# Forgetting attention with 64-row score matmuls, one division on ScalarE and early exponential tables; latent attention with the second head's queries ahead of the first exponentials

## The chip, the core and the metric

The program runs on one core of a Trainium2 chip. The metric is the device time of one execution in microseconds (us); lower is better. The changed kernel is timed against the kernel before on the same chip.

## The reference, cut to what matters

The model is two decoder layers on 256 rows of width 1024. Layer 0 mixes with forgetting attention (16 heads of 64), layer 1 with latent attention (16 heads). Each layer has two gated feed-forward halves around the mixer and a gated input embedding behind them, with a layer norm after each step.

```python
def fox_mixer(x, w_in, b_f, w_o):
    h = x @ w_in                      # queries, keys, values, and 16 gate logits
    cum = jnp.cumsum(jax.nn.log_sigmoid(f_logit), axis=1).transpose(0, 2, 1)
    s = jnp.einsum('bqhd,bkhd->bhqk', qb, k) * FOX_HEAD_DIM ** -0.5
    s = s + cb[:, :, :, None] - cum[:, :, None, :]     # then causal softmax, times v, times w_o
def mla_mixer(x, w_dq, q_norm, w_uq, w_o, k_nope, k_rope, v, cos, sin):
    c_q = rms_norm(x @ w_dq, q_norm)
    q = jnp.einsum('bsc,chd->bshd', c_q, w_uq)         # 128 plain and 64 rotated columns a head
    s = jnp.einsum('bqhd,bkhd->bhqk', qn, k_nope) + jnp.einsum('bqhr,bkr->bhqk', qr, k_rope)
for i in range(DEPTH):
    x = post_norm(x, 0.5 * swiglu(x, ffn1_w_in[i], ffn1_w_out[i]), ln_g[i, 0], ln_b[i, 0])
    ...
```

## The kernel before, in words

**Number format.** Every product is made of three float32r matmuls: both operands are split into a high part (a copy on ScalarE that rounds) and a low part (a subtraction on VectorE), and the products high-high, high-low and low-high are added up in PSUM. `parts` does it for an activation, `Stream.split` for a weight that a DMA has brought into a `raw` buffer. So each block of weights costs ScalarE and VectorE one pass each before TensorE can use it.

**What sets the order.** The engines' programs are written out by hand: what stands earlier in the code is earlier in each engine's queue, and an engine works through its queue in order. Only the weight splits are placed by a planner: `pump`, called after every three matmuls, puts the next split in if its own estimate of the engines' clocks allows. `S.hold` forbids that. A split can be cut in two (`ahead`, `later`): its ScalarE half is queued at one place (L172) and its VectorE half at another (L176). PSUM has three rings of banks: `y` (4), `h` (2) and `tr` (2).

**Forgetting attention** (`fox`, L807). The values and the gates come first. The gate chain (`s1`, `s2`, `s3`) uses an exponential (L859) and a logarithm (L866) on ScalarE, then sends the sums of the logarithms through DRAM and back as `fall`, and masks it on GpSimd (`mask_fall`, L898). Heads are worked in 8 pairs j. For each pair: `gen_k` makes the keys of two heads in 128 rows (head 0 in rows 0 to 63, head 1 in 64 to 127), `gen_q` the queries; `QK` the scores; `softmax` the bias and row minimum (VectorE, L952), four exponentials with their sums (ScalarE, L962), the reciprocals of the sums (VectorE, L969), four divisions (GpSimd, L973); `T` transposes the weights on TensorE (L986, L471), `AV` multiplies by the values. The loop (L1033) issues, on TensorE: `gen_k(j+1)`, `T(j-1)`, `QK(j)`, `gen_q(j+1)`, `AV(j-1)`. Behind the loop come the output products `O`, a block of queries at a time, the first block's layer norm, and the transposes `XT(0)` of the normed block, ahead of the last `O(7, 1)`.

**The scores before.** The keys are kept in `kz` with zeros in the other head's rows (two memsets, L845 and L846, and four half copies, L918 and L920), so that one matmul over all 128 rows gives both heads:

```python
for n, (i, jj) in enumerate(((0, 0), (0, 1), (1, 0))):
    self.mm(pairs(sb[0][:, 0:256]), q[:, i, 0:128], pairs(k[:, jj])[:, :, 0:128], n == 0, n == 2)
for n, (i, jj) in enumerate(((0, 0), (0, 1), (1, 0))):
    self.mm(sb[1], q[:, i, 128:256], k[:, jj], n == 0, n == 2)
```

**Latent attention** (`mla`, L1146). The query latent is normed in `dq` (`rms_scale`: a square with sum on ScalarE, L1089; mean plus epsilon on GpSimd, L1090; a power on GpSimd, L1091; the scaling on VectorE, L1165). Then come values `V`, rotated queries `q_rope` and `rotate`, and their transposes `rope_T`. Heads are worked one by one: `QK(h)`, `softmax(h)` (VectorE, L1288), `T(h-1)`, `exps(h)` (ScalarE, L1297), `divide(h)` (VectorE L1305, GpSimd L1307), and `gen(h+1)` (`gen_k`, `gen_q`: keys and queries of the next head in one bank, split into `qk`). For head 0 the keys of head 1 are made ahead of the loop, and `gen_q(1)` stands behind `divide(0)`. Two blocks of values, `V(2, 0)` and `V(2, 1)`, are split just ahead of the loop into a tile of the ring `g4` (g in the trace) and into `qq`.

Of the kernel before, what the change touches and what calls it, by code (L numbers as in the profile page):

```python
# [10 lines left out]
F32 = mybir.dt.float32  # L11
F32R = mybir.dt.float32r
AF = mybir.ActivationFunctionType
ALU = mybir.AluOpType
# [367 lines left out]
class Trunk:  # L382
# [33 lines left out]
    def setup(self):  # L416
        nc = self.nc
        one = lambda shape, dt, name: self.tl(shape, dt, name, 1)
        self.x = [one([128, D], F32, f"x{t}") for t in range(2)]
        self.ident = one([128, 128], F32, "ident")  # L420
        self.mask = one([128, 384], F32, "mask")
        self.mhalf = one([128, 1], F32, "mhalf")
        self.xT = one([128, 2, 2, 8, 128], F32R, "xT")
# [11 lines left out]
        nc.gpsimd.memset(self.mhalf, -0.5)  # L435
        nc.scalar.activation(warm, self.mhalf, AF.Silu)
# [370 lines left out]
    def fox(self, li):  # L807
# [39 lines left out]

        f, e, u, r, ab = (fs[fr, 256 * i : 256 * i + 256] for i in range(5))
        sc = fs[:, 1280:1536]
# [2 lines left out]
        def gates():  # L852
# [56 lines left out]
        st, PT = {}, {}  # L909
        OT = [self.own([128, 4, 2, 256], F32R, tag) for tag in ("ota", "otb")]  # L910

        def gen_k(j):
            ps = self.bank("h")
            ws(("fk", j), ps[:, 0:256], {0: S.split_now} if j >= 2 else {}, j >= 2)
            o = kz[:, j % 2]
            part = [(slice(64 * s, 64 * s + 64), slice(256 * s, 256 * s + 256)) for s in range(2)]
            for r, c in part:
                nc.scalar.activation(o[r, 0, c], ps[r, 0:256], AF.Copy)  # L918
            for r, c in part:
                nc.vector.tensor_tensor(o[r, 1, c], ps[r, 0:256], o[r, 0, c].bitcast(F32), op=ALU.subtract)  # L920
            self.S.busy(act=600, dve=600)

        def gen_q(j):
            ps = self.bank("h")
            ws(("fq", j), ps[:, 0:256], {}, j >= 2)
            o = qq[:, j % 2]
            self.parts(o[:, 0, :], o[:, 1, :], ps[:, 0:256])

        def QK(j, ring):
            sb = [self.bank(ring) for _ in range(2)]  # L930
            q, k = qq[:, j % 2], kz[:, j % 2]
            pairs = lambda ap: ap.rearrange("p (s c) -> p s c", s=2)
            for n, (i, jj) in enumerate(((0, 0), (0, 1), (1, 0))):
                self.mm(
                    pairs(sb[0][:, 0:256]), q[:, i, 0:128], pairs(k[:, jj])[:, :, 0:128], n == 0, n == 2
                )
            for n, (i, jj) in enumerate(((0, 0), (0, 1), (1, 0))):
                self.mm(sb[1], q[:, i, 128:256], k[:, jj], n == 0, n == 2)
            st[j] = sb

        def softmax(j):
# [5 lines left out]
            seg = ((0, 128), (128, 384))  # L947
            S2 = [[sb[q][:, w * s : w * s + w] for q, w in enumerate((128, 256))] for s in range(2)]
# [21 lines left out]
            for s in range(2):  # L970
                for q, (c0, c1) in enumerate(seg):
                    i = 2 * s + q
                    nc.gpsimd.tensor_scalar(  # L973
                        P[s][:, c0:c1], P[s][:, c0:c1], su[:, i : i + 1], 1.0, op0=ALU.mult, op1=ALU.mult
                    )
            if j < 7:
                mask_fall(j + 1)
            st[j] = P

        def T(j):  # L980
# [39 lines left out]
        gen_q(0)  # L1020
        y = [[None] * 2 for _ in range(2)]

        def O(k, t):
            w = self.use(("fo", k))
            if k == 0:
                y[t] = [self.bank("y") for _ in range(2)]
            for n in range(2):
                self.mm3(
                    y[t][n], lambda i: OT[k // 4][:, k % 4, i, 128 * t : 128 * t + 128],
                    lambda i: w[:, i, 512 * n : 512 * n + 512], k == 0, k == 7,  # L1030
                )

        for j in range(8):  # L1033
# [16 lines left out]
            softmax(j)  # L1050
            if j < 7:
                gen_q(j + 1)
            else:
                O(2, 0)
                S.split_now()
                O(3, 0)
            if j >= 1:
# [26 lines left out]
    def rms_scale(self, src, n, junk):  # L1084
# [61 lines left out]
    def mla(self, li):  # L1146
# [116 lines left out]
        def gen(h):  # L1263
            gen_k(h)
            gen_q(h)
# [111 lines left out]
        rope_T(0, 0)  # L1377
        split_v = V(2, 0, "y", later=True)
        rope_T(1, 0)
        if not self.rec:  # L1380
            split_v()
        V(2, 1, "y", "qq")
        for h in range(16):
            S.hold = True
            QK(h)
            softmax(h)
            if h >= 1:
                T(h - 1)
            exps(h)
            if h >= 1:  # L1390
                T_low(h - 1)
            divide(h)
            if h == 0:
                gen_q(1)
            elif h < 15:
                gen(h + 1)
            S.hold = False
            if h == 0:
# [118 lines left out]
```

## Time and profile before

| | |
|---|---|
| median of 3 runs | 1081.13 us (1080.95 to 1082.05) |
| profiled execution, its own time | 1080.49 us |
| its span, first to last instruction | 1078.7 us |
| TensorE matmul busy | 1064.0 us (99%), 7050 matmuls |
| VectorE busy | 711.2 us (66%) |
| ScalarE busy | 541.8 us (50%) |
| GpSimd busy | 86.9 us (8%) |
| read from HBM | 199.95 MB, 186 GB/s over the span |

The busy time of TensorE says little by itself, since a matmul's end is modelled and overlaps its successor. The useful reading is the time from the start of one group of matmuls to the start of the next: it shows what a group costs, and where TensorE stood still. PEld is TensorE's loading of weights, DVE is VectorE, ACT is ScalarE, POOL is GpSimd. A row of the timeline has the start, the length of the merged group, engine, line, operation, tiles, shapes and count, and in brackets the idle time before it with what ended it. Consecutive rows of one engine that do the same are merged, also across two weights.

### The profile page before, as it was taken

How to read it: one execution, taken by the hardware profiler on the slowest of the kernel's cores; microseconds unless marked ns; L12 is line 12 of the kernel's file. 1: busy time of each engine (PE TensorE's matmuls, PEld its weight loads, DVE VectorE, ACT ScalarE, POOL GpSimd, SP SyncE). 2: the span in 40 equal slices, each digit the busy share in tenths (PEclk: the TensorE clock that was granted, in tenths of full speed). 3: DMA queues.
4: the chain of work that ended last, by engine and by line, in shares of the span. 5: the costliest groups of instructions: out<-in, count | busy, mean ns of one | idle time of the engine just before them, and what ended most of it. 6: DMA issues, size and time to landing. Idle time of an engine off the chain costs nothing. (4 is left out here: it accounts for less than half of the span.)

```text
span 1078.7 us, 17453 instructions
## 1 busy us (share of the span) xinstructions
PE 1064.0 (99%) x7050; PEld 966.6 (90%) x7050; DVE 711.2 (66%) x979; ACT 541.8 (50%) x797; POOL 86.9 (8%) x143
## 2 busy tenths in 40 slices
PE   9999999999999999999999999999999999999996
PEld 6989999889889989998899898988999889898985
DVE  5765545778797545458977454488886985454567
ACT  5564433557656435453555343345766474444431
POOL 0000000333300000000330000011111100000000
PEclk9999999999999999999999999999999999999998
DMA  9886653455358866545387564344473678555502
GB/s 286 283 295 228 198 193 98 157 196 197 96 173 281 266 229 195 195 144 188 104 297 264 195 196 158 98 106 132 147 221 127 196 248 289 187 181 188 187 1 78
DMA packets 151616, 202.14 MB, mean 187 GB/s; under 512 B 12000, under 2 KB 128752, under 8 KB 151536
## 3 DMA queue, kind: packets, MB, share of 16 engines
q1 hardware_dynamic: 151536, 201.04, 56.9%
q8 instruction: 55, 0.90, 0.3%
q14 instruction: 25, 0.20, 0.1%
HBM read 199.95 MB, written 1.06 MB: 186 GB/s over the span
## 5 line engine op out<-in xcount | busy, mean ns | idle before, releaser
L165 DVE TENSOR_TENSOR hl<-raw,hl 128x1024 fp32r<-128x1024 f32 (+3 forms) x286 | 330.1, 1174 | 160.6 <-ACT hl L164 159.4
L164 ACT ACTIVATE hl<-raw 128x1024 fp32r<-128x1024 f32 (+3 forms) x286 | 283.9, 1017 | 196.3 <-PE y L467 85.5
L467 PE MATMUL h<-xT,hl 128*128 128x256 f32 x2064 | 242.4, 277 | 0.0
L467 PEld LDWEIGHTS h<-xT,hl 128*128 128x128 f32 x2064 | 238.7, 188 | 0.7
L467 PE MATMUL y<-hl,g 128*128 128x512 f32 x804 | 186.6, 390 | 0.0
L467 PEld LDWEIGHTS y<-hl,g 128*128 128x128 f32 x804 | 150.1, 188 | 30.7
L467 PE MATMUL tr<-xT,hl 128*128 128x256 f32 x840 | 98.9, 277 | 0.0
L467 PEld LDWEIGHTS tr<-xT,hl 128*128 128x128 f32 x840 | 96.9, 188 | 0.1
L467 PE MATMUL h<-hl,xT 128*128 128x512 f32 (+1 forms) x396 | 94.5, 388 | 0.9 <-DVE hl L165 0.9
L467 PEld LDWEIGHTS h<-hl,xT 128*128 128x128 f32 x396 | 71.9, 188 | 17.2 <-DVE hl L165 2.7
L539 POOL TENSOR_TENSOR rs<-ve,mhalf 128x1 f32<-128x1 f32 x16 | 15.2, 950 | 820.3 <-DVE ve L538 806.7
L467 PE MATMUL y<-hl,xT 128*128 128x512 f32 (+2 forms) x276 | 57.8, 363 | 0.0
L467 PEld LDWEIGHTS y<-hl,xT 128*128 128x128 f32 x276 | 47.5, 188 | 7.4
L477 DVE TENSOR_TENSOR g<-P,g 128x512 fp32r<-128x512 f32 x36 | 24.9, 693 | 34.5 <-ACT g L476 34.5
L476 ACT ACTIVATE g<-P 128x512 fp32r<-128x512 f32 x36 | 22.7, 632 | 40.0 <-DVE P L646 29.0
L165 DVE TENSOR_TENSOR otb<-raw,otb 128x1024 fp32r<-128x1024 f32 (+1 forms) x20 | 24.0, 1202 | 19.4 <-ACT otb L164 19.4
L467 PE MATMUL y<-hl,ota 128*128 128x512 f32 x144 | 36.2, 394 | 0.0
L165 DVE TENSOR_TENSOR qk<-raw,qk 128x1024 fp32r<-128x1024 f32 x21 | 25.8, 1229 | 15.0 <-ACT qk L164 15.0
L476 ACT ACTIVATE xT<-tr 128x512 fp32r<-128x512 f32 x32 | 17.8, 595 | 31.7 <-PE tr L471 31.4
L467 PE MATMUL tr<-xT,otb 128*128 128x256 f32 x264 | 31.7, 276 | 0.0
L164 ACT ACTIVATE otb<-raw 128x1024 fp32r<-128x1024 f32 (+1 forms) x20 | 20.8, 1040 | 21.0 <-PE tr L467 10.6
L164 ACT ACTIVATE qk<-raw 128x1024 fp32r<-128x1024 f32 x21 | 22.2, 1058 | 17.7 <-PE tr L467 6.6
(240 smaller groups left out, 1390.0 us busy)
## 6 DMA issues: line engine op xcount, KB each, us to landing
raw<-in_ffn_w_in_dram SPq DMA_DIRECT2D x172, 512.0 KB, 5.0
raw<-in_ffn_w_out_dram SPq DMA_DIRECT2D x44, 1024.0 KB, 5.0
raw<-in_fox_w_in_dram SPq DMA_DIRECT2D x12, 1024.0 KB, 5.3
raw<-in_ple_w_gate_dram SPq DMA_DIRECT2D x8, 1024.0 KB, 4.9
raw<-in_mla_w_o_dram SPq DMA_DIRECT2D x8, 1024.0 KB, 5.3
gb<-in_ln_g_dram SPq DMA_DIRECT2D x8, 512.0 KB, 7.4
gb<-in_ln_b_dram SPq DMA_DIRECT2D x8, 512.0 KB, 8.2
raw<-in_fox_w_o_dram SPq DMA_DIRECT2D x4, 1024.0 KB, 6.1
```

Of the source, the lines that this page charges most:

```text
L164: nc.scalar.activation(hi[:, c], src[:, c], AF.Copy)
L165: nc.vector.tensor_tensor(lo[:, c], src[:, c], hi[:, c].bitcast(F32), op=ALU.subtract)
L467: self.nc.tensor.matmul(out, lhsT, rhs, start=start, stop=stop)
L476: self.nc.scalar.activation(hi, src, AF.Copy)
L477: self.nc.vector.tensor_tensor(lo, src, hi.bitcast(F32), op=ALU.subtract)
L539: nc.gpsimd.tensor_tensor(rs, ve, self.mhalf, op=ALU.pow)
```

## The change

In forgetting attention the zeros go: queries and keys of a pair lie in one tile `qk`, and each score matmul runs over the 64 rows of one head, the two heads in turn and each into a bank of its own. There are 12 such matmuls for a pair of heads (6 with 128 columns, 6 with 256) where there were 6 (3 with 256, 3 with 512). Keys are split by one copy and one subtraction. The fourth division of a pair (head 1, second block of queries) goes from GpSimd to ScalarE, behind `gen_q(j+1)`. A one-column exponential behind the gates' logarithm, and another one ahead of latent attention's first heads, load ScalarE's table for the exponentials there. The last output product `O(7, 1)` is cut in two, and `XT(0)` stands between its halves. `rms_scale` adds epsilon on ScalarE. In latent attention `gen_q(1)` stands ahead of `exps(0)`, and the splits of `V(2, 0)` and `V(2, 1)` stand behind `divide(0)`.

```diff
@@ fox
-        kz = self.own([128, 2, 2, 512], F32R, "qk")
-        qq = self.tl([128, 2, 2, 256], F32R, "qq", 1)
+        qk = self.own([128, 2, 2, 512], F32R, "qk")
-        nc.gpsimd.memset(kz[64:128, :, :, 0:256].bitcast(F32), 0.0)
-        nc.gpsimd.memset(kz[0:64, :, :, 256:512].bitcast(F32), 0.0)
...
                 nc.scalar.activation(ab, u, AF.Ln)
+                nc.scalar.activation(bf[:, 1:2], self.mhalf, AF.Exp)
...
+        half = (slice(0, 64), slice(64, 128))
+        seg = ((0, 128), (128, 384))
+        def gen(j, key, c0, at={}, hold=False):
+            ps = self.bank("h")
+            ws((key, j), ps[:, 0:256], at, hold)
+            o = qk[:, j % 2]
+            self.parts(o[:, 0, c0 : c0 + 256], o[:, 1, c0 : c0 + 256], ps[:, 0:256])
...
-            for n, (i, jj) in enumerate(((0, 0), (0, 1), (1, 0))):
-                self.mm(sb[1], q[:, i, 128:256], k[:, jj], n == 0, n == 2)
+            for q, (c0, c1) in enumerate(seg):
+                for n, (i, jj) in enumerate(((0, 0), (0, 1), (1, 0))):
+                    for s in range(2):
+                        self.mm(
+                            sb[s][:, c0:c1], o[half[s], i, 128 * q : 128 * q + 128],
+                            o[half[s], jj, 256 : 256 + c1 - c0], n == 0, n == 2,
+                        )
...
+                    if i < 3:
+                        nc.gpsimd.tensor_scalar(
+                            P[s][:, c0:c1], P[s][:, c0:c1], su[:, i : i + 1], 1.0, op0=ALU.mult, op1=ALU.mult
+                        )
...
+        def divide_last(j):
+            P, su = st[j]
+            nc.scalar.activation(P[1][:, 128:384], P[1][:, 128:384], AF.Copy, scale=su[:, 3:4])
...
             if j < 7:
                 gen_q(j + 1)
+                divide_last(j)
...
-        for k in range(2, 8):
-            if k == 7:
-                self.XT(0)
+        for k in range(2, 7):
             O(k, 1)
+        O(7, 1, (0,))
+        self.XT(0)
+        O(7, 1, (1,))
@@ rms_scale
-        nc.gpsimd.tensor_scalar(ve, ss, 1.0 / n, RMS_EPS, op0=ALU.mult, op1=ALU.add)
+        nc.scalar.activation(ve, ss, AF.Identity, bias=self.eps, scale=1.0 / n)
@@ mla
         rotate(0, 0)
+        nc.scalar.activation(self.tl([128, 1], F32, "ss", 2), self.mhalf, AF.Exp)
...
-        if not self.rec:
-            split_v()
-        V(2, 1, "y", "qq")
+        late = [split_v, V(2, 1, "y", "qq", later=True)]
         for h in range(16):
...
+            else:
+                gen_q(1)
             exps(h)
...
             divide(h)
-            if h == 0:
-                gen_q(1)
+            if h == 0 and not self.rec:
+                for f in late:
+                    f()
```

**TensorE around the first two pairs' scores, before.** `qk` and `qq` are the keys and queries, `h<-xT` the making of further queries and keys, `tr<-ident,P` the transposes `T(0)`:

```order
L467 MATMUL h<-xT,hl_1918 128x256 x24
L467 MATMUL y<-qk,qq 128x256 x3
L467 MATMUL y<-qk,qq 128x512 x3
L467 MATMUL h<-xT,hl_1981 128x256 x24
L467 MATMUL h<-xT,hl_2015 128x256 x24
L986 MATMUL tr<-ident,P 128x128 x4
L471 MATMUL tr<-ident,P 128x128 x2
```

The same place on TensorE in the changed kernel:

```order
L469 MATMUL h<-xT,hl_1917 128x256 x24
L469 MATMUL y<-qk 128x128 x6
L469 MATMUL y<-qk 128x256 x6
L469 MATMUL h<-xT,hl_1980 128x256 x24
L469 MATMUL h<-xT,hl_2015 128x256 x24
L989 MATMUL tr<-ident,P 128x128 x4
L473 MATMUL tr<-ident,P 128x128 x2
```

The order of the groups stays; only the scores' own rows change, from 3 and 3 to 6 and 6 matmuls of half the columns.

**ScalarE from the first keys to the first pair's weights, before.** `L962` are the four exponentials, `hl_2232` a weight split, `PT` the copy behind `T(0)`:

```order
L918 ACTIVATE qk<-h 64x256 x2
L962 ACT_TABLE_LOAD
L962 ACTIVATE P,su<-y,nm 128x128
L962 ACTIVATE P,su<-y,nm 128x256
L962 ACTIVATE P,su<-y,nm 128x128
L962 ACTIVATE P,su<-y,nm 128x256
L476 ACTIVATE qq<-h 128x256
L172 ACTIVATE hl_2232<-raw 128x1024
L918 ACTIVATE qk<-h 64x256 x2
L476 ACTIVATE PT<-tr 128x512
```

The same stretch of ScalarE's queue in the changed kernel:

```order
L478 ACTIVATE qk<-h 128x256
L959 ACTIVATE P,su<-y,nm 128x128
L959 ACTIVATE P,su<-y,nm 128x256
L959 ACTIVATE P,su<-y,nm 128x128
L959 ACTIVATE P,su<-y,nm 128x256
L478 ACTIVATE qk<-h 128x256
L980 ACTIVATE P<-P,su 128x256
L172 ACTIVATE hl_2234<-raw 128x1024
L478 ACTIVATE qk<-h 128x256
L478 ACTIVATE PT<-tr 128x512
```

The table load is gone from this place (it stands behind the logarithm now), the half copies have become whole ones, and a division (L980) stands ahead of the weight split.

**ScalarE around latent attention's first head, before.** `xT` are the rotated queries' transposes, `g` and `qq` the values of `V(2, 0)` and `V(2, 1)`, `qk` the second head's queries and keys, `hl` weight splits:

```order
L1230 ACTIVATE xT<-tr 64x512 x4
L476 ACTIVATE g_7194<-y 128x512
L476 ACTIVATE qq<-y 128x512
L1297 ACT_TABLE_LOAD
L1297 ACTIVATE P,su<-tr,nm 128x128
L1297 ACTIVATE P,su<-tr,nm 128x256
L476 ACTIVATE qk<-h 128x512
L164 ACTIVATE hl_7249<-raw 128x768
L164 ACTIVATE hl_7260<-raw 128x1024
L1317 ACTIVATE PT<-tr 128x384
```

The same stretch of ScalarE's queue in the changed kernel:

```order
L1236 ACTIVATE xT<-tr 64x512 x4
L478 ACTIVATE qk<-h 128x512
L1303 ACTIVATE P,su<-tr,nm 128x128
L1303 ACTIVATE P,su<-tr,nm 128x256
L478 ACTIVATE g_7228<-y 128x512
L478 ACTIVATE qq<-y 128x512
L164 ACTIVATE hl_7292<-raw 128x768
L1323 ACTIVATE PT<-tr 128x384
```

The second head's copy has moved from behind the exponentials to ahead of them, the two value copies from ahead to behind, and the second weight split of 1024 columns is no longer placed here.

More of the change, by code (lines that the diff above doesn't have):

```diff
@@ L422, in setup @@
         self.mhalf = one([128, 1], F32, "mhalf")
+        self.eps = one([128, 1], F32, "eps")
         self.xT = one([128, 2, 2, 8, 128], F32R, "xT")
@@ L435, in setup @@
         nc.gpsimd.memset(self.mhalf, -0.5)
+        nc.gpsimd.memset(self.eps, RMS_EPS)
         nc.scalar.activation(warm, self.mhalf, AF.Silu)
@@ L910, in fox @@
         OT = [self.own([128, 4, 2, 256], F32R, tag) for tag in ("ota", "otb")]
-        def gen_k(j):
[L913 to L921, printed above, removed]
+        half = (slice(0, 64), slice(64, 128))
[5 more added lines that the diff above has]
+            self.parts(o[:, 0, c0 : c0 + 256], o[:, 1, c0 : c0 + 256], ps[:, 0:256])
+        def gen_k(j):
+            gen(j, "fk", 256, {0: S.split_now} if j >= 2 else {}, j >= 2)
         def gen_q(j):
[L924 to L927, printed above, removed]
+            gen(j, "fq", 0, {}, j >= 2)
         def QK(j, ring):
             sb = [self.bank(ring) for _ in range(2)]
-            q, k = qq[:, j % 2], kz[:, j % 2]
-            pairs = lambda ap: ap.rearrange("p (s c) -> p s c", s=2)
-            for n, (i, jj) in enumerate(((0, 0), (0, 1), (1, 0))):
[L934 to L937, printed above, removed]
-                self.mm(sb[1], q[:, i, 128:256], k[:, jj], n == 0, n == 2)
+            o = qk[:, j % 2]
+            for q, (c0, c1) in enumerate(seg):
[5 more added lines that the diff above has]
+                        )
             st[j] = sb
@@ L946, in softmax @@
             P = [pair[:, 384 * s : 384 * s + 384] for s in range(2)]
-            seg = ((0, 128), (128, 384))
-            S2 = [[sb[q][:, w * s : w * s + w] for q, w in enumerate((128, 256))] for s in range(2)]
+            S2 = [[sb[s][:, c0:c1] for c0, c1 in seg] for s in range(2)]
             for s in range(2):
@@ L1021, in fox, with O @@
         y = [[None] * 2 for _ in range(2)]
-        def O(k, t):
+        def O(k, t, ns=(0, 1)):
             w = self.use(("fo", k))
@@ L1026, in O @@
                 y[t] = [self.bank("y") for _ in range(2)]
-            for n in range(2):
+            for n in ns:
                 self.mm3(
@@ L1052, in fox @@
                 gen_q(j + 1)
+                divide_last(j)
             else:
                 O(2, 0)
+                divide_last(j)
                 S.split_now()
@@ L1392, in mla @@
             divide(h)
-            if h == 0:
-                gen_q(1)
-            elif h < 15:
+            if h == 0 and not self.rec:
+                for f in late:
+                    f()
+            if 0 < h < 15:
                 gen(h + 1)
```

4 lines of the change are left out of this document (1 added, 3 removed).

## The prediction, made before the changed kernel ran

> **What bounds the kernel now.** I read the page first, for what is busy.
>
> ```profile
> span 1078.7 us, 17453 instructions
> ...
> PE 1064.0 (99%) x7050; PEld 966.6 (90%) x7050; DVE 711.2 (66%) x979; ACT 541.8 (50%) x797; POOL 86.9 (8%) x143
> ```
>
> TensorE sets the time; no other engine is above 66%. A change can pay only in two ways: fewer or shorter steps on TensorE, or places where TensorE stands still. For the second I read the waits of TensorE (who was waited for, total us, times, longest):
>
> ```profile
> PE tr L986 <- POOL P L973: 1.1, 1, 1.1
> ...
> PE tr L467 <- ACT qk L476: 0.6, 1, 0.6
> ...
> PE tr L467 <- DVE qk L477: 0.4, 1, 0.4
> ```
>
> These are single events. One is the first transposes of forgetting attention, the other two the second head's scores in latent attention, and the change edits both places. Since a matmul's end is modelled, the waits understate the loss; I take it from starts in the timeline. TensorE in forgetting attention, the first two pairs of heads and a later one:
>
> ```profile
> 226.67 5.61 PE L467 MATMUL h<-xT,hl 128*128 128x256 f32 x48
> 232.42 1.13 PE L986 MATMUL tr<-ident,P 128*128 128x128 f32 x3
> 234.63 0.33 PE L986 MATMUL tr<-ident,P 128*128 128x128 f32 x1 [1.08 <-POOL P L973]
> ...
> 234.94 1.30 PE L467 MATMUL y<-qk,qq 128*128 128x256 f32 x6
> ...
> 239.97 2.89 PE L467 MATMUL h<-xT,hl 128*128 128x256 f32 x24
> 242.70 0.60 PE L986 MATMUL tr<-ident,P 128*128 128x128 f32 x4
> ...
> 243.27 1.29 PE L467 MATMUL y<-qk,qq 128*128 128x256 f32 x6
> 244.40 0.85 PE L467 MATMUL h<-xT,hl 128*128 128x256 f32 x6
> ```
>
> Undisturbed, 24 matmuls of 256 columns take 242.70 - 239.97 = 2.73 us (0.114 each), six transposes of 128 columns 243.27 - 242.70 = 0.57 (0.095 each), one pair's scores 244.40 - 243.27 = 1.13. So the first transposes were due at 226.67 + 48 x 0.114 = 232.13 and the next scores 0.57 later, at 232.70. They began at 234.94: 2.24 us are lost once.
>
> **The change part by part.** *The first pair's softmax.* ScalarE, VectorE and GpSimd ahead of those transposes:
>
> ```profile
> 228.66 1.28 ACT L962 ACT_TABLE_LOAD   x1 [2.06 <-DVE nm L952]
> ...
> 231.46 0.21 ACT L962 ACTIVATION_READ_ACCUMULATOR P<-y,nm 128x1 f32 x1
> 231.55 0.39 ACT L476 ACTIVATE qq<-h 128x256 fp32r<-128x256 f32 x1
> 231.70 0.18 DVE L969 RECIPROCAL su<-su 128x4 f32<-128x4 f32 x1 [2.74 <-ACT P L962]
> ...
> 231.99 2.59 POOL L973 TENSOR_SCALAR P<-P,su 128x128 f32<-128x128 f32 x4 [4.29 <-DVE su L969]
> ```
>
> The table load stands between the row minimum and the first exponential; asked for behind the logarithm, its 1.28 us leave this chain. Exponentials then end at about 230.3, the reciprocal starts at 230.4, the divisions at 230.7. Three of the four stay on GpSimd. In a later pair four of them take
>
> ```profile
> 239.70 1.63 POOL L973 TENSOR_SCALAR P<-P,su 128x128 f32<-128x128 f32 x4 [4.40 <-DVE su L969]
> ```
>
> 0.41 each, so three end at 231.9, ahead of 232.13. The fourth, on ScalarE, waits for the reciprocal behind the copy of the next queries: 230.3 + 0.39 + about 0.4 (the same width as that copy) = 231.1. Queued behind it are a weight split and the next keys' copy, neither wanted by TensorE for some 2 us. So of 2.24 I count 2.1 as gained, and 1.3 to 2.3 as possible: the lower end if GpSimd is as slow as at 231.99 (0.65 each). The load itself is paid at its new place, behind the logarithm. There it delays copies and weight splits, and ScalarE makes it up before the first keys:
>
> ```profile
> 220.37 0.79 ACT L918 ACTIVATE qk<-h 64x256 fp32r<-64x256 f32 x2 [2.15 <-PE h L467]
> ```
>
> It had waited 2.15 us for TensorE there, more than 1.28 plus a small activation. I cost it at nothing; without that cover it would cost up to 1.5.
>
> *The two memsets, the half copies of the keys, the epsilon.* All lie on GpSimd, ScalarE and VectorE, where the waits above name none of them. Behind the epsilon on ScalarE stands a weight split of 512 columns that is 0.2 later for it. Nothing, with 0.2 either way.
>
> *Transposes between the halves of the last output product.* The end of forgetting attention:
>
> ```profile
> 302.80 4.24 PE L467 MATMUL y<-hl,otb 128*128 128x512 f32 x18
> ...
> 306.10 1.41 DVE L544 SCALAR_TENSOR_TENSOR x<-x,rs,gb 128x512 f32<-128x512 f32 x2
> ...
> 306.99 1.29 PE L471 MATMUL tr<-ident,x 128*128 128x128 f32 x8
> ...
> 308.04 1.65 PE L467 MATMUL y<-hl,otb 128*128 128x512 f32 x6
> ...
> 309.53 1.53 PE L467 MATMUL h<-hl,xT 128*128 128x512 f32 x6
> ```
>
> Eighteen matmuls of 512 columns took 4.19 us, 0.233 each. The eight transposes took 308.04 - 306.99 = 1.05 where 8 x 0.095 = 0.76 would do, because the norm's second half is finished at 306.10 + 1.41 = 307.51. Three matmuls later (0.70), at 307.69, nothing is missing: 0.29 gained. Late next is the transposed row itself, wanted by the feed-forward at 307.69 + 0.76 + 0.70 = 309.15 instead of 309.53. A copy and a subtraction of that width take 0.59 and 0.69 (rows below), so the low half is there at about 309.5, and the third matmul wants it at 309.6. I take 0.3, between 0 and 0.4.
>
> *Latent attention, second head.* The same stretch on all engines:
>
> ```profile
> 742.58 0.69 DVE L477 TENSOR_TENSOR g<-y,g 128x512 fp32r<-128x512 f32 x1
> ...
> 743.32 2.27 PE L467 MATMUL y<-hl,fall 128*128 128x512 f32 x9
> 743.79 0.29 DVE L1288 CUSTOM_DVE_ANT_0 tr<-tr,mask 128x128 f32<-128x128 f32 x1
> ...
> 744.69 0.37 ACT L1297 ACTIVATE P<-tr,nm 128x128 f32<-128x128 f32 x1 [1.17 <-DVE nm L1288]
> ...
> 745.50 0.59 ACT L476 ACTIVATE qk<-h 128x512 fp32r<-128x512 f32 x1
> ...
> 745.98 1.80 ACT L164 ACTIVATE hl<-raw 128x768 fp32r<-128x768 f32 x2
> 745.98 0.83 POOL L1307 TENSOR_SCALAR P<-P,su 128x128 f32<-128x128 f32 x2 [14.44 <-DVE su L1305]
> ...
> 746.15 0.33 PE L467 MATMUL tr<-qk 128*128 128x128 f32 x1 [0.56 <-ACT qk L476]
> 746.86 2.17 DVE L165 TENSOR_TENSOR hl<-raw,hl 128x768 fp32r<-128x768 f32 x2
> ...
> 746.88 0.44 PE L467 MATMUL tr<-qk 128*128 128x128 f32 x2 [0.40 <-DVE qk L477]
> ...
> 748.02 0.49 PE L471 MATMUL tr<-ident,P 128*128 128x128 f32 x3
> ...
> 749.06 1.23 PE L467 MATMUL h<-fall,hl 128*128 128x256 f32 x9
> ```
>
> The second head's scores were due at 743.32 + 9 x 0.233 = 745.42 and the transposes behind them (nine steps in 748.02 - 746.88 = 1.14, one more 0.1) at 746.66. They came at 748.02: 1.36 lost. The cause is the queues: VectorE subtracts values (742.58) ahead of the first head's minimum (743.79), so the exponentials are late, and ScalarE copies `qk` only behind them, at 745.50. The table load plays no part here, since ScalarE was already idle for 1.17 when the minimum came; asking for it early gains nothing. In the changed order VectorE does the minimum from 742.6 (0.9 us, as from 743.79 to 744.69), ScalarE copies `qk` as soon as TensorE has it, about 743.5 to 744.1, and VectorE's subtraction (0.69) ends by 744.8: before 745.42. The exponentials wait behind that copy; they run from 744.1 to 744.9 (0.81 as before), and the divisions, which ended 1.31 after them, are done at 746.2: before 746.66. Late next are the weights for the third head's queries, which now stand behind the two deferred value splits: ScalarE's two copies of 0.59 to about 746.0 and its 768 columns (768/1792 of 1.80 = 0.77) to 746.8, VectorE's share of 2.17 (0.93) to 747.8. TensorE reaches them at 746.66 + (749.06 - 748.02) = 747.70, and needs the low part two steps later, at 747.93. I take 1.25, between 0.7 and 1.4.
>
> *The scores over 64 rows.* The only edit of TensorE's own steps, eight times over, and the one whose price the trace does not show: every matmul in it has 128 rows. The steps above say that halving the columns does not halve the time: 0.095 at 128 columns, 0.114 at 256. If the two heads' matmuls, which use different rows of the array and different banks, run side by side, a pair costs 3 x 0.095 + 3 x 0.114 = 0.63. Against that stands the turn from 128 rows to 64 and back. Its nearest row is a matmul's length against its step:
>
> ```profile
> L467 PE MATMUL h<-xT,hl 128*128 128x256 f32 x2064 | 242.4, 277 | 0.0
> ```
>
> 277 ns, less the step of 114, is 0.163 that a successor normally hides; shown twice, 0.33, so 0.96. I take 0.90, nearer to the upper end, since no row shows such a turn to be free: (1.13 - 0.90) x 8 = 1.8 gained, between 1.4 and 4.0. If they do not run side by side, twelve steps cost 6 x 0.095 + 6 x 0.114 = 1.25 and with both turns 1.58: 1.0 to 3.6 lost.
>
> The Trainium skill, TensorEngine Tiling (Array Packing), section Key Properties, speaks for the first and warns of the second: tiles of rows can load weights and multiply in parallel, but a change of tiling mode drains the engine. No run here shows either yet. The Trainium skill, TensorE: Matmul & The Clock Gate, section LDWEIGHTS, says that a weight load costs by its columns (columns over 1.2, so 107 ns for 128), whatever its rows; if loads went one by one, twelve of them would be an estimated 1.28 us, by which the sum would come out as in the second rival below. The flat steps of 0.095 and 0.114 agree with that rule.
>
> *The sum.* 2.1 + 0.3 + 1.25 + 1.8 = 5.5 us off the profiled execution's own 1080.49 (span 1078.7 and 1.8 around it), so 1075.0. That execution stands 0.6 below the median of 1081.13, against which the changed kernel will be seen: 1075.6.
>
> **The rivals.** *The stalls move instead of going* (7%). The changed queues put a division and two value splits ahead of weight splits; if GpSimd stays at 0.65 a division and the third head's weights come 0.6 late, half of the 3.65 stays: about 1077.5. For it speaks only the slow row at 231.99, against it the later row of 1.63 for four.
>
> *The score matmuls go one by one* (27%). Weight loads take turns, 1.25 to 1.58 a pair. The stalls still go: -3.65 + 1.0 to 3.6, so 1078.5 to 1081.1, at the middle 1079.8. For it: PEld is 90% busy and small matmuls cost a nearly constant step. Against it: the two heads' rows and banks are disjoint.
>
> *Every turn of the rows empties the array* (6%), slower. Twelve matmuls at their full length of 277 ns would make 3.3 us a pair, 17.5 in all, and 1095. It decides from a mean step of 0.156: 12 x 0.156 = 1.87 a pair, 0.74 over 1.13, eats the 3.65 and another 2.2. No row speaks for it; the full hiding of 0.163 between 128-row matmuls speaks against.
>
> *The change does not do what it says* I give nothing of its own: the order shows no table load left at the exponentials of either attention.
>
> **How the numbers follow.** About 0.2% (2.2 us) is what a measurement of this kernel can tell from no change. Forecast, 60%: side by side, stalls gone, 1075.6; its own range is 1073.0 (all upper ends: 4.1 of stalls, 4.0 of scores) to 1077.7 (all lower ends: 2.0 and 1.4). The upper end of the whole is 1081.1, the last of the one-by-one case. Left out are the 6% of the emptied array and some 10% of misjudged bounds on both sides. Faster: 60 + 7 and about 6 of the 27, 73%. Within 0.2%: the other 21. Slower: 6.
>
> **What would show it.** Right: between the first scores and the first transposes no table load on ScalarE, the next scores about 0.6 behind the first transposes; no wait at the second head's scores of latent attention; the score groups of forgetting attention at 0.7 to 1.0 us a pair, two matmuls starting almost together. Wrong: score groups of 1.25 or more with evenly spaced starts; a new wait at the third head's queries (weights from VectorE), or at the first transposes with ScalarE's division as the releaser.

## The result, and the profile after

The changed kernel took 1085.11 us (median of 20 runs, 1079.07 to 1086.93); the kernel before took 1081.67 beside it (20 runs, 1080.52 to 1083.14). The ratio is 1.0027, with a 95% interval of 1.0017 to 1.0036: slower by a quarter of a per cent, clear of the noise. The profiled executions are 1084.97 us (span 1083.2) and 1080.49 (span 1078.7). The forecast was 1075.6, with 1081.1 as its upper end.

The page of the changed kernel has TensorE busy for 6.9 us more:

```profile
span 1083.2 us, 17503 instructions
...
PE 1070.9 (99%) x7098; PEld 972.3 (90%) x7098; DVE 708.6 (65%) x971; ACT 543.6 (50%) x803; POOL 74.1 (7%) x130
```

Only 48 matmuls were added, so its steps must have become longer. Before looking for those, I check the places that the prediction named. TensorE around the first two pairs of heads and a later pair (columns as before: start, us, instruction, count):

```profile
227.81 5.73 PE L469 MATMUL h<-xT,hl 128*128 128x256 f32 x48
...
233.38 0.60 PE L989 MATMUL tr<-ident,P 128*128 128x128 f32 x4
233.81 0.38 PE L473 MATMUL tr<-ident,P 128*128 128x128 f32 x2
234.12 0.95 PE L469 MATMUL y<-qk 64*128 64x128 f32 x12
...
241.74 0.60 PE L989 MATMUL tr<-ident,P 128*128 128x128 f32 x4
242.17 0.38 PE L473 MATMUL tr<-ident,P 128*128 128x128 f32 x2
242.49 0.95 PE L469 MATMUL y<-qk 64*128 64x128 f32 x12
243.37 3.01 PE L469 MATMUL h<-xT,hl 128*128 128x256 f32 x24
246.21 1.21 PE L469 MATMUL y<-PT,g 128*128 128x512 f32 x6
247.26 3.00 PE L469 MATMUL h<-xT,hl 128*128 128x256 f32 x24
250.10 0.60 PE L989 MATMUL tr<-ident,P 128*128 128x128 f32 x4
```

The first transposes follow the 48 matmuls without a wait, and the six take 234.12 - 233.38 = 0.74 where they had taken 234.94 - 232.42 = 2.52. That stall is gone. The chain that leads to it, on ScalarE, VectorE and GpSimd, has no table load:

```profile
229.87 0.37 ACT L959 ACTIVATE P<-y,nm 128x128 f32<-128x128 f32 x1 [2.45 <-DVE nm L949]
...
231.62 0.18 DVE L966 RECIPROCAL su<-su 128x4 f32<-128x4 f32 x1 [1.01 <-ACT P L959]
231.84 0.51 ACT L980 ACTIVATE P<-P,su 128x256 f32<-128x256 f32 x1
...
231.91 1.18 POOL L971 TENSOR_SCALAR P<-P,su 128x128 f32<-128x128 f32 x3 [2.73 <-DVE su L966]
```

The score groups take 243.37 - 242.49 = 0.88 instead of 1.13. To see what a pair costs in all, these are rows of the later pair in the kernel before that the prediction does not show:

```profile
243.14 0.38 PE L471 MATMUL tr<-ident,P 128*128 128x128 f32 x2
...
247.12 1.21 PE L467 MATMUL y<-PT,g 128*128 128x512 f32 x6
248.17 3.00 PE L467 MATMUL h<-xT,hl 128*128 128x256 f32 x24
251.01 0.60 PE L986 MATMUL tr<-ident,P 128*128 128x128 f32 x4
```

The scores now begin 242.49 - 242.17 = 0.32 behind the start of the last two transposes, where it was 243.27 - 243.14 = 0.13. The two groups of 24 matmuls behind the scores take 2.84 each; before, in each of the next pairs too, one of the two took 2.72 or 2.73 and the other 2.83 or 2.84. From one pair's transposes to the next it is 250.10 - 241.74 = 8.36, before 251.01 - 242.70 = 8.31, and 8.31 to 8.34 in the next three pairs. So the shorter scores come with 0.19 lost ahead of them and some 0.1 in the groups behind: about 0.04 is lost a pair.

The second head of latent attention:

```profile
746.32 2.26 PE L469 MATMUL y<-hl,fall 128*128 128x512 f32 x9
748.42 0.44 PE L469 MATMUL tr<-qk 128*128 128x128 f32 x3
...
749.57 0.49 PE L473 MATMUL tr<-ident,P 128*128 128x128 f32 x3
...
750.61 0.64 PE L469 MATMUL h<-fall,hl 128*128 128x256 f32 x4
```

The scores come at 746.32 + 9 x 0.233 = 748.42, to the hundredth when they are due, and the next transposes 1.15 later: the 1.36 lost there are gone too. The end of forgetting attention, after and then before:

```profile
297.83 0.62 PE L469 MATMUL y<-hl,otb 128*128 128x512 f32 x2
298.64 1.19 PE L469 MATMUL y<-hl,otb 128*128 128x512 f32 x4 [0.19 <-DVE otb L1018]
299.67 2.90 PE L469 MATMUL y<-hl,ota 128*128 128x512 f32 x12
302.42 4.93 PE L469 MATMUL y<-hl,otb 128*128 128x512 f32 x21
307.18 1.03 PE L473 MATMUL tr<-ident,x 128*128 128x128 f32 x8
307.97 0.94 PE L469 MATMUL y<-hl,otb 128*128 128x512 f32 x3
308.75 1.64 PE L469 MATMUL h<-hl,xT 128*128 128x512 f32 x6
```

```profile
298.47 1.74 PE L467 MATMUL y<-hl,otb 128*128 128x512 f32 x6
300.05 2.91 PE L467 MATMUL y<-hl,ota 128*128 128x512 f32 x12
```

The eight transposes take 0.79 instead of 1.05: 0.26 gained. The product of the last pair's result now waits: six matmuls take 299.67 - 297.83 = 1.84, before 300.05 - 298.47 = 1.58. That is 0.26 lost.

So the mixers gained about what was forecast for them without the scores. The loss is in the feed-forwards, which the change does not touch. Two of layer 0's products and one of layer 1's, before and after:

```profile
336.06 8.42 PE L467 MATMUL h<-xT,hl 128*128 128x256 f32 x72
...
366.08 16.50 PE L467 MATMUL y<-hl,g 128*128 128x512 f32 x72
...
404.74 11.04 PE L467 MATMUL h<-xT,hl 128*128 128x256 f32 x96
...
951.71 11.04 PE L467 MATMUL h<-xT,hl 128*128 128x256 f32 x96
```

```profile
335.57 8.73 PE L469 MATMUL h<-xT,hl 128*128 128x256 f32 x72
...
366.75 16.48 PE L469 MATMUL y<-hl,g 128*128 128x512 f32 x72
...
405.81 11.47 PE L469 MATMUL h<-xT,hl 128*128 128x256 f32 x96
...
954.05 11.47 PE L469 MATMUL h<-xT,hl 128*128 128x256 f32 x96
```

The same 96 matmuls without a wait take 11.04 or 11.47. From the first of the 72 to the 512-column products stand 264 matmuls: 366.08 - 336.06 = 30.02 before, 366.75 - 335.57 = 31.18 after. That is 113.7 and 118.1 ns a matmul. It is not the clock: 8 us inside such a run, before and then after (window; us; busy us and matmuls (x); the granted clock stands behind GpSimd's column):

```profile
407.00:415.00 8.00, 8.00 (x73) 8.00 (x72) 4.51 (x5) 3.50 (x4) 0.00 (x0) 1.00 0.70 222
```

```profile
407.00:415.00 8.00, 8.00 (x71) 8.00 (x70) 4.37 (x4) 3.95 (x5) 0.00 (x0) 1.00 0.70 219
```

The four feed-forwards hold twelve such stretches of 264 or 288 matmuls (the expectations call them long runs), whose moving operand is `xT` (the activation's transposes) and whose stationary ones are mostly the weight tiles `hl`. Each keeps one median step from start to end, whichever weight tile is read. Before, all twelve stood at 113 ns; after, seven did and five (from 336, 394, 445, 943 and 993 us) stood at 118. At 118.1 - 113.7 = 4.4 ns more a matmul a stretch at 118 costs 1.16 or 1.27 us more, the five 6.2. Along the program (starts from the timelines):

| step on TensorE | before | after | after less before |
|---|---|---|---|
| first scores, forgetting attention | 225.62 | 226.93 | +1.3 |
| second pair's scores | 234.94 | 234.12 | -0.8 |
| first feed-forward block behind the mixer | 309.53 | 308.75 | -0.8 |
| first long run of layer 0's second feed-forward | 336.06 | 335.57 | -0.5 |
| rotated queries of heads 8 to 15, latent attention | 743.32 | 746.32 | +3.0 |
| third head's queries | 749.06 | 750.61 | +1.6 |
| the 96 matmuls of layer 1 shown above | 951.71 | 954.05 | +2.3 |
| span | 1078.7 | 1083.2 | +4.5 |

Most of the first +1.3 arose within the first 24 us. Three kernels of the study that differ from before by an unused tile alone, and have no stretch at 118 ahead of the scores, have the first scores at 226.38 to 226.60. So some +0.8 to +1.0 of it is likely the start-up of the two profiled executions and not the change. Then the mixers take off 2.1 and 1.4, and the stretches at 118 add 3.7 in layer 0 and 2.5 in layer 1.

### The profile page after: what moved, and what is told of

Same layout as the page of the kernel before. It is cut to its first block, busy times and chain, and to the rows that moved or that the text cites. A ratio compares the mean times of both kernels' runs of the same rounds, so it can differ in the third digit from the quotient of the medians.

```text
span 1083.2 us, 17503 instructions
## 1 busy us (share of the span) xinstructions
PE 1070.9 (99%) x7098; PEld 972.3 (90%) x7098; DVE 708.6 (65%) x971; ACT 543.6 (50%) x803; POOL 74.1 (7%) x130
## 5 line engine op out<-in xcount | busy, mean ns | idle before, releaser
L469 PE MATMUL h<-xT,hl 128*128 128x256 f32 x2064 | 246.4, 279 | 0.0
L469 PEld LDWEIGHTS h<-xT,hl 128*128 128x128 f32 x2064 | 241.2, 188 | 1.2 <-DVE P L613 0.2
```

The source lines that it names most:

```text
L469: self.nc.tensor.matmul(out, lhsT, rhs, start=start, stop=stop)
```

## The experiments

Three theories were held against each other, with these letters in the expectations. R: the 64-row matmuls leave TensorE in a slower way of working. S: any shift in time between the engines picks anew which stretches stand at 118. A: the new `eps` tile does it by its place. In the programs as built a column of 128 x 1 takes 32 bytes a partition; it is allocated ahead of `xT` and moves `xT`, the weight tiles and most later tiles by 32 bytes. (The queries' tile that the 64-row scores no longer need moves `qq` and a few small tiles by more, in every kernel with those scores.)

**The changed kernel with the scores of before.** Keys padded with zeros, 128-row scores, memsets, all else as changed:

```diff
-        qk = self.own([128, 2, 2, 512], F32R, "qk")
+        kz = self.own([128, 2, 2, 512], F32R, "qk")
+        qq = self.tl([128, 2, 2, 256], F32R, "qq", 1)
+        nc.gpsimd.memset(kz[64:128, :, :, 0:256].bitcast(F32), 0.0)
```

> The changed kernel with the scores of the kernel before (zero-padded keys, 128 rows); all else of the change stays. Theory S (step): the time is lost in the feed-forwards, where a 256-column matmul steps at 113.3 or at 117.8 ns, picked by TensorE's phase when a run of them begins; a slow run of 264 or 288 costs 1.2 to 1.3 us, and no edit in itself makes it. By S slow runs may come or go here, and the time is about 1078.5 plus 1.2 to 1.3 for each slow run. Theory R (rows): the 64-row matmuls leave TensorE slower behind them; by R no run behind forgetting attention is slow, and the time is about 1078.5.

1086.44 us, ratio 1.0033 (1.0022 to 1.0044). Four stretches at 118, from 35, 557, 941 and 992 us, without a 64-row matmul in the program. R falls.

**The scores alone.** The kernel before with only the 64-row scores and whole key copies:

```diff
-        kz = self.own([128, 2, 2, 512], F32R, "qk")
+        qk = self.own([128, 2, 2, 512], F32R, "qk")
```

> The kernel before with the 64-row scores alone. The scores' groups with their turns should cost about what the 128-row ones cost (0 to 0.4 us more over eight pairs). Theory R: slow runs of 117.8 ns appear behind forgetting attention as in the changed kernel, 1085 to 1088. Theory S: any number of slow runs, so 1081 to 1088 in steps of 1.2 to 1.3, not tied to the scores.

1080.12 us, ratio 0.9982 (0.9973 to 0.9990), all twelve stretches at 113. The gain is not in the score groups. ScalarE here:

```profile
226.24 0.38 ACT L476 ACTIVATE qk<-h 128x256 fp32r<-128x256 f32 x1 [1.39 <-PE h L467]
226.64 1.28 ACT L956 ACT_TABLE_LOAD   x1
228.25 0.37 ACT L956 ACTIVATE P<-y,nm 128x128 f32<-128x128 f32 x1 [0.33 <-DVE nm L946]
```

The table load is still at its old place in the queue, but starts right behind the copy, at 226.64 instead of 228.66. In the program as built, waits included, one sees why. Before:

```
L962 ACT_TABLE_LOAD [waits DVE_49]
L962 ACTIVATE P,su<-y,nm 128x128 [waits PE_49]
```

With 64-row scores:

```
L956 ACT_TABLE_LOAD
L956 ACTIVATE P,su<-y,nm 128x128 [waits DVE_49]
```

Before, the first exponential waited for VectorE and for TensorE, and the wait for VectorE stood ahead of the load. With the 64-row scores only one wait is left, it stands on the exponential, and the load is free. So this edit alone takes most of the first stall away: the first six transposes take 0.95 here, 2.52 before and 0.74 with the whole change.

**Other edges in the feed-forward.** Dummy transposes of the identity stand ahead of some of the stretches, and `EDGE` says how many. Three of them get one more, in the changed kernel and in the kernel before:

```diff
-EDGE = {("ffn1", 5): 4, ("ffn1", 8): 4, ("ffn2", 5): 1, ("ffn2", 8): 4}
+EDGE = {("ffn1", 5): 4, ("ffn1", 8): 4, ("ffn2", 2): 1, ("ffn2", 5): 2, ("ffn2", 8): 5}
```

> The changed kernel with other numbers of the dummy transposes that stand ahead of runs of the second feed-forward (1, 2 and 5 where there were 0, 1 and 5 minus 1), 0.3 us of work in each of the two layers. Theory S: the set of slow runs in the second feed-forwards changes, so the time moves by steps of 1.2 to 1.3, between 1079 and 1086. Theory R: still four or five slow runs, 1085.6.

> The kernel before with the same other numbers of dummy transposes, nothing else. Theory S: runs of the second feed-forwards turn slow although no mixer was touched, 1082.5 to 1088. Theory R: all runs stay at 113.3 ns, and the time is 1081.7 plus 0.6 for the transposes.

The changed kernel with them: 1083.34 us, ratio 1.0014 (1.0005 to 1.0024), four stretches at 118, three of which are slow without the additions too. The kernel before with them: 1081.95, ratio 1.0 (0.9991 to 1.0009), none at 118. This shift in time alone does not bring the longer step into the kernel before, which speaks against S as the whole cause.

**The move alone.** The kernel before with an unused tile ahead of `xT`; no instruction differs:

```diff
         self.mhalf = one([128, 1], F32, "mhalf")
+        self.pad = one([128, 1], F32, "pad")
         self.xT = one([128, 2, 2, 8, 128], F32R, "xT")
```

> The kernel before with one unused tile of 32 bytes a partition ahead of the transposed activations; no instruction is added, only addresses of the tiles behind it move by 32 bytes, as the epsilon tile moves them in the changed kernel. Theory A (addresses): where the operands of TensorE lie decides how often its 256-column matmuls step at 117.8 instead of 113.3 ns; by A slow runs appear here and the time is 1084 to 1088. Theory S (step by timing alone): no instruction and no time changes, so no slow runs, 1081.7 as before.

1086.91 us, ratio 1.0054 (1.0038 to 1.0070). In its trace, that of its fastest execution (1083.95, the others up to 1089.60), two stretches stand at 118, the 96 matmuls of layer 1 among them:

```profile
953.07 11.47 PE L468 MATMUL h<-xT,hl 128*128 128x256 f32 x96
```

**The change without the move.** All edits, with epsilon in a second column of `mhalf`, whose 32 bytes have room for it:

```diff
-        self.mhalf = one([128, 1], F32, "mhalf")
-        self.eps = one([128, 1], F32, "eps")
+        mh = one([128, 2], F32, "mhalf")
+        self.mhalf, self.eps = mh[:, 0:1], mh[:, 1:2]
```

> The whole change, with epsilon put into the unused second column of an existing tile, so that no tile's address moves by the 32 bytes. Theory A: no slow runs but by chance, and the time is what the profile of the changed kernel leaves without them, 1077.5 (to 1079). Theory S or any of the other edits as the cause: slow runs as in the changed kernel, 1085.

1078.26 us, ratio 0.9969 (0.9957 to 0.9981), all stretches at 113:

```profile
950.57 11.04 PE L469 MATMUL h<-xT,hl 128*128 128x256 f32 x96
```

These two settle that the place does it. The edits are worth 3.05 us against the 1081.31 of the kernel before, timed beside it, and 32 bytes of placement took away more than that. A holds; this version beats both kernels.

A trace shows one execution, though. The changed kernel's twenty lie between 1079.07 and 1086.93 at a granted clock of 0.997 to 0.998 throughout, some six stretches apart. So the place seems to set how often a stretch is slow, and which ones are slow seems to be drawn anew in each execution, which leaves room for timing as in S. No second execution was traced to show it.

**The change with other moves of all tiles** (a second unused tile behind `eps`: 64, 96 and 128 bytes in all):

> The whole change with a second unused tile, so that the addresses move by 64 bytes and lie within a block of 64 bytes as in the kernel before. Theory A in the form that the place within 64 bytes decides: few slow runs, 1077.5 to 1079. Theory A in a form that any move spoils a tuned order, or theory S: slow runs, 1082 to 1087.

> The changed kernel with another unused tile of 64 bytes ahead of xT, so that everything stands 96 bytes above where it stood in the kernel before (the changed kernel: 32). Theory P2 (xT and weights both on a multiple of 64 bytes lets some long runs fall into the step of 118 ns, both at an odd multiple of 32 does not): like the changed kernel, 1083 to 1087 us with some long runs at 118. Theory Q (no such rule, every move draws a new set of slow runs): anything from 1078 to 1087.

> The changed kernel with everything 128 bytes above where it stood in the kernel before, both xT and the weights again at an odd multiple of 32. Theory P2: like the whole change without a move, 1077.5 to 1079.5 us, no long run at 118 or one. Theory Q: anything from 1078 to 1087. The move by 64, also odd, was between at 1081.4, which already speaks for Q or for a weaker rule.

1081.40 us, ratio 0.9995 (0.9986 to 1.0003), two stretches at 118; 1084.37, 1.0028 (1.0019 to 1.0037), four; 1084.09, 1.0023 (1.0014 to 1.0033), four. No rule of odd and even multiples of 32 comes out (P2 falls); each joint move that was tried puts some stretches at 118, and never the same set. This fits Q, but with one trace a kernel it does not show that the move picks the set.

**The distance between the two operands.** In the kernel before, first `xT` alone is moved by 32 bytes (`mhalf` allocated behind it), then, by an unused tile behind `xT`, all other tiles by 32, 64, 128, 512 and 1024:

```diff
         self.xT = one([128, 2, 2, 8, 128], F32R, "xT")
+        self.pad = one([128, 1], F32, "pad")
```

> The kernel before with mhalf allocated behind xT instead of ahead of it: xT alone moves, by 32 bytes down; every later tile and every instruction stays. xT is the moving operand of the long 256-column runs of the feed-forwards, the weight tiles are the stationary one. Theory X (the place of xT decides TensorE's step): some of the twelve long runs at 118 ns a step, 1083 to 1088 us. Theory W (the place of the weight tiles and other later buffers decides): all at 113, within 1 us of the kernel before. Rival: any move of any tile that leaves the relative distance of xT to the weights changed does it; then this kernel and the next are both slow.

> The kernel before with an unused tile of 32 bytes behind xT: xT stays where it was, all later tiles (rope, the weight tiles, the splits' raw buffers) move by 32 bytes up. Theory X (the place of xT): all twelve long runs at 113 ns, within 1 us of the kernel before. Theory W (the place of the later tiles): some at 118, 1083 to 1088 us.

> The kernel before with an unused tile of 64 bytes behind xT: xT stays, all later tiles move by 64 bytes. Theory P (what counts is whether xT and the weight tiles stand alike within 64 bytes): within 1.5 us of the kernel before, long runs at 113 ns. Theory D (any change of their distance does it): all twelve long runs at 117 to 119 ns, about 1098 us, as when xT or the rest moved by 32.

> The kernel before with 128 unused bytes behind xT. If the distance from xT to the weight tiles counts within 128 bytes: all long runs at 113 ns, within 1.5 us of the kernel before. If any change of that distance makes all of them slow: 1098 to 1102 us.

> The kernel before with 512 unused bytes behind xT. If the distance counts within a period that divides 512: within 1.5 us of the kernel before. If any change does it: 1098 to 1102 us.

> The kernel before with 1024 unused bytes behind xT. If the distance counts within a period that divides 1024 (a row of 256 columns is 1024 bytes a partition): within 1.5 us of the kernel before. If any change does it: 1098 to 1102 us. A time in between or below the kernel before would say that the slow steps are drawn anew at each distance.

| distance changed by | us | ratio to before (95%) | stretches at 117 to 121 ns |
|---|---|---|---|
| 32 (`xT` moved) | 1099.26 | 1.0161 (1.0147 to 1.0175) | 12 of 12 |
| 32 (the rest moved) | 1098.61 | 1.0156 (1.0142 to 1.0170) | 12 |
| 64 | 1102.20 | 1.0190 (1.0176 to 1.0204) | 12 |
| 128 | 1094.53 | 1.0113 (1.0100 to 1.0127) | 9 |
| 512 | 1080.97 | 0.9996 (0.9985 to 1.0007) | 0 |
| 1024 | 1082.07 | 1.0001 (0.9992 to 1.0010) | 0 |

The same 96 matmuls with `xT` moved by 32, and with the rest moved by 512:

```profile
968.11 11.55 PE L467 MATMUL h<-xT,hl 128*128 128x256 f32 x96
```

```profile
954.20 11.04 PE L468 MATMUL h<-xT,hl 128*128 128x256 f32 x96
```

I had expected only one of the two operands to matter. Both moves by 32 cost the same, so neither place by itself decides but the distance of the two. It matters for 32, 64 and 128 bytes and not for 512 or 1024, so a rule within 64 or 128 falls (P), and one within 512 fits. Which of the later tiles counts was not separated: `raw` moves along with the weight tiles. Unlike a joint move, a distance changed by 32 or 64 bytes puts every stretch at the longer step.

**Parts of the change, without a move.** The scores of before; the latent part undone; the early exponential behind the logarithm and the division on ScalarE undone:

```diff
-                nc.scalar.activation(bf[:, 1:2], self.mhalf, AF.Exp)
...
-            nc.scalar.activation(P[1][:, 128:384], P[1][:, 128:384], AF.Copy, scale=su[:, 3:4])
```

> The change without the 64-row scores and without the move of addresses. Theory A: no slow runs, 1077.5 to 1079, and the difference to the whole change without the move is what the 64-row scores are worth in it (0 to 0.5 us either way). Theory S: slow runs as in the first experiment, 1084 to 1087.

> The whole change without a moved tile (epsilon in a spare column), less its latent-attention part: second head's queries behind the exponentials again, value splits ahead, no early exponential there. The latent part is worth 1.45 us in the trace, 1.25 by the prediction: so 1.2 to 1.5 us above the kernel with the whole change in the same place, at 0.9980 to 0.9984 of the kernel before. If the change's gain outside forgetting attention is an accident of placement, no difference.

> The whole change without a moved tile, less the early exponential behind the logarithm and the division on ScalarE: the table load stands ahead of the first exponentials again and GpSimd does four divisions. If these two carry the 2.1 us counted for forgetting attention's first transposes: 2 us above the whole change in the same place, 0.9988 to 0.9992 of the kernel before. The run of the scores alone had lost most of that stall without them: by that, 0 to 0.5 us above, at 0.9970 to 0.9975.

With the scores of before 1078.86 us, ratio 0.9975 (0.9965 to 0.9985); without the latent part 1080.02, 0.9984 (0.9976 to 0.9993); without the early exponential and the division 1078.05, 0.9968 (0.9956 to 0.9980). The whole change had 0.9969. So the latent part is worth some 1.6 us by the ratios; it shows in the trace without it, then in that of the whole change, as 749.02 - 744.34 = 4.68 against 746.52 - 743.27 = 3.25, 1.43 more:

```profile
744.34 2.27 PE L469 MATMUL y<-hl,fall 128*128 128x512 f32 x9
747.15 0.33 PE L469 MATMUL tr<-qk 128*128 128x128 f32 x1 [0.55 <-ACT qk L478]
...
749.02 0.49 PE L473 MATMUL tr<-ident,P 128*128 128x128 f32 x3
```

```profile
743.27 2.26 PE L469 MATMUL y<-hl,fall 128*128 128x512 f32 x9
745.37 0.44 PE L469 MATMUL tr<-qk 128*128 128x128 f32 x3
...
746.52 0.49 PE L473 MATMUL tr<-ident,P 128*128 128x128 f32 x3
```

The trace without the latent part has something else: its first stretch, from 36 us, stands at 118. These are 96 of its matmuls, there and in the whole change without the move:

```profile
55.49 11.47 PE L469 MATMUL h<-xT,hl 128*128 128x256 f32 x96
```

```profile
54.37 11.04 PE L469 MATMUL h<-xT,hl 128*128 128x256 f32 x96
```

The two kernels do not differ ahead of latent attention, neither in instructions nor in places. So the longer step comes at the old place too, only rarely: in 1 of 84 stretches in the traces of the seven kernels without a move, against 25 of 84 in the seven with a joint move. Some of the 1.6 us may be such stretches; the 1.43 above is not.

The other two parts come out within the intervals of the whole, because either of them removes the first stall by itself, the scores all but 0.2 of it: the early exponential by taking the load away, the scores by taking its wait away. Having both pays once. For the last kernel I had named 2 us by the prediction's reasoning, and 0 to 0.5 by the run of the scores alone; the miss of the first shows it.

## Why the prediction was wrong

The failed step is *the two memsets, the half copies of the keys, the epsilon*: "Nothing, with 0.2 either way". I costed the epsilon by its instructions and asked which engine waits for them. Its tile was not costed at all. Adding 32 bytes ahead of every operand of the feed-forwards put five of twelve stretches at 118 ns a step; the move alone cost 5.6 us (1086.91 against 1081.31), the change gained 3.05 without it and lost 3.44 with it (1085.11 against 1081.67). Where 5.5 were forecast as gained, the move thus accounts for some 6.5 of the miss, and the steps below for the other 2.45. The range had no term for anything that the change does not touch. Only 6% were given to a slower kernel, and to another mechanism.

The other steps, in the prediction's order:

- *The first transposes*, forecast 2.1 of 2.24: all of it gained. Divisions on GpSimd took 1.18 / 3 = 0.39 each, close to the later row's 0.41, not 0.65. That the load was the cause is right; that it had to be moved is not, since its wait was the matter.
- *Transposes between the halves*, forecast 0.3: 0.26 gained at the transposes, and 0.26 lost earlier at the last pair's product. Without the early exponential and the division that product takes 299.01 - 297.45 = 1.56 in its trace, so it is those that cost this; by which step was not followed. The two cancel.
- *Latent attention*, forecast 1.25: 1.43 to 1.45 (748.02 - 743.32 = 4.70 before, 749.57 - 746.32 = 3.25 after). Nothing was late next.
- *The scores*, forecast 1.8 with 0.90 a pair: the group itself took 0.88, but the turns are not in it, 0.19 stand ahead and some 0.1 more in the groups behind, and the pair comes to about 0.04 more than before, 0.3 in all. I had put a price for turns into the 0.90 in the belief that the scores alone would be shorter (0.63); they are 0.88 without the turns. This term is mis-sized by 2.1. The flat steps, which the prediction took to agree with the rule on weight loads that it cites, do not quite: 0.095 is shorter than a load by that rule.

Of the rivals, matmuls one by one falls (twelve in 0.88 is less than 1.25), so does the emptied array (about 0.04 lost a pair, not 0.74), and the stalls moved only by that 0.26. Without the move, the 3.65 forecast of stalls less the 0.3 for the scores and the 0.26 make 3.1; 3.05 was measured.

## What to carry to other kernels

Count what an edit does to memory as well as to the queues: a new or a removed tile moves every tile behind it. Where a kernel is slower in a part that the edit leaves alone, compare the mean step of the same group of matmuls in both traces, at the same granted clock, and then move a tile without changing an instruction. Look at the spread of the times too: one trace shows one execution. And before moving a table load, read which wait it carries; two edits that lift the same wait pay once.

## What the runs showed of the hardware

- The step of 256-column float32r matmuls is not one number. At a granted clock of 1.00 it is 113 ns or 117 to 121 ns, constant over a stretch of 264 or 288. Changing the distance between the moving operand `xT` and the tiles behind it, the stationary operands among them, by 32, 64 or 128 bytes brought the longer step to 12, 12 and 9 of twelve stretches, by 512 or 1024 to none (others were not tried). Moving both together brought it to 25 of 84, against 1 of 84 without a move. What picks the stretches in that case stays open, and so does the mechanism in memory: no row of a profile names it.
- Products of 512 columns with `xT` as the stationary operand hardly show it: 24 of them (from 326.89 us before, from 333.43 with `xT` moved by 32) took 5.50 and 5.60. The products of `g` and `hl` (72 in 16.50 and 16.48) do not tell, since those two keep their distance in all these kernels.
- Matmuls over two halves of the rows do run side by side: twelve in 0.88 us, 0.073 each, less than the 0.095 of one at 128 columns; the two of a pair start 3 to 6 ns apart in the trace. The turn from 128 rows to 64 costs 0.19 ahead of them; what the turn back costs is not separated from the groups behind. The Trainium skill, TensorEngine Tiling (Array Packing), section Key Properties, says both, that tiles work in parallel and that a change of mode drains the engine; the trace agrees with the first, and the 0.19 fits the second.
